# Where the seven-product quads stand in the down projection: the first after eight weight tiles, then one every four

## The chip, the cores and the metric

The kernel runs on one core of a Trainium2 chip. A core has a matrix engine (TensorE, here PE, with PEld for its weight loads), a vector engine (DVE), a scalar engine (ACT), GpSimd (POOL) and a queue that mostly starts transfers (SP). PE multiplies 128x128 weight blocks with up to 512 columns and adds into PSUM banks. The engines run side by side and wait for one another through semaphores. The metric is the device time of one execution in microseconds (us); the kernel before has a median of 2102.93 us over 3 runs (2102.6 to 2103.97).

## The reference

One transformer-like block on 256 tokens of width 2048, in float32: a feed-forward part, a mixer, and a second feed-forward part, each with a root-mean-square norm ahead and behind and a residual. Only the feed-forward parts matter here:

```python
D_FF = int(math.ceil(8 * D_MODEL / 3 / 256)) * 256        # 5632

def _swiglu(x, w_gate, w_up, w_down):
    return (jax.nn.silu(x @ w_gate) * (x @ w_up)) @ w_down

f = _swiglu(_rmsnorm(h, ln_ffn1_pre[l]), ffn1_gate[l], ffn1_up[l], ffn1_down[l])
h = h + MACARON_WEIGHT * _rmsnorm(f, ln_ffn1_post[l])
```

The down product takes the hidden values (256 x 5632) times `w_down` (5632 x 2048). The mixer (projections, a recurrent branch, a pooling branch) stands between the two feed-forward parts and is not touched.

## The kernel before, in words

**Precision.** Each float32 operand is split into a high part (a cast to the fast format fp32r) and a low part (the remainder). A product is three matmuls: high by high (line 158), low weights by high (159), high weights by low (160). So every weight tile passes through three engines before PE: a DMA from SP's queue brings it, ACT casts it (tile `wH`, line 134), DVE subtracts the cast from it (tile `wL`, line 135). The raw tiles `w32` have 4 buffers, `wH` and `wL` 5 each (lines 35 and 36): a new DMA waits until the low part of the tile four places before is done, a new cast until PE has finished the tile five places before.

**The feed-forward part.** `ffn` goes through 11 blocks of 512 hidden columns: gate, then up, then the product of the two. `shuffle_split` brings each block into the layout that the down product needs, with 16 small copies on ACT (line 493), a cast to the high part (496) and a subtraction on DVE (497). Then `post` calls `seven` twice, for output columns 0 to 1023 and 1024 to 2047.

**`seven`** forms two 512-column halves, `f` and `l`, for two halves of the tokens. The inner dimension has 44 rows of 128. The last 32 go the plain way, two at a time: `pair` loads one tile (two rows by 512 columns) and does four products of three matmuls, 12 matmuls in all. This text counts such tiles from 0; there are 16 for `f` and 16 for `l`. The first 12 rows go by a Strassen-like scheme, two at a time, in six quads: `quad` does seven products (21 matmuls) in place of eight, into banks named `ms` or `mm`. Each quad takes

- four DMAs of 256 KB into two `w32` buffers (line 279),
- three DVE operations that form differences of the weights, `t13` (283) and `t24` (285, 286),
- four splits, each a cast on ACT (293) and a subtraction on DVE (294): the direct weights, half a tile more, `t13` and `t24`,
- sums of the input, which `sums` makes for two quads at a time: DVE 218 to 228, a cast on ACT (230), DVE 231. In the first call of `seven` they are made for quads 1 and 2 at its start, and for the next ones when the first and third quad are issued. The second call uses them again.

**The order.** In the loops of `seven` a quad is issued behind the tiles whose numbers stand in `QUADS` (line 48): the first list for the `f` loop, the second for the `l` loop, `False` for the first call and `True` for the second. Behind the last quad `merge` combines the seven banks. DMAs stand in SP's queue in the order in which they are issued; on PE, ACT and DVE a scheduler orders the instructions when the program is built, and the splits and weight differences have a high priority (lines 133, 282, 292), the sums and `shuffle_split` none.

Of the kernel before, what the change touches and what calls it, by code (L numbers as in the profile page):

```python
# [44 lines left out]
WARM = 12  # L45
TB = 4
NQ = 6
QUADS = {False: ((4, 9, 14), (2, 5, 8)), True: ((2, 5, 8, 11, 14), (1,))}

ROWS = [("ln_mix_pre", 16), ("ln_ffn2_pre", 16), ("mu", 26), ("w0", 8), ("a0", 8),  # L50
        ("k_k", 8), ("k_a", 8)]
# [3 lines left out]
class Block:  # L55
# [179 lines left out]
    def seven(s, w, cf, cl, at, KT, T, sm, ev_first, ev_last, trail):  # L235
# [29 lines left out]
        def pair(k, c0, b):  # L265
            keep(s.load_w(w, k, 2, c0, 512))
            for i in range(2):
                for h in range(2):
                    mul(f"{b}{h}", rows(k + i, h), ws[k + i])
# [43 lines left out]
        for i, k in enumerate(range(K0, KT, 2)):  # L313
            pair(k, cf, "f")
            if i in QUADS[trail][0]:
                quad(next(q))
# [16 lines left out]
        for i, k in enumerate(tiles):  # L333
            pair(k, cl, "l")
            if i in QUADS[trail][1]:
                quad(next(q))
# [1017 lines left out]
```

## Time and profile before

| | |
|---|---|
| median of 3 runs | 2102.93 us |
| profiled execution, its own time | 2103.1 us |
| its span, first to last instruction | 2101.4 us |
| PE, PEld, DVE, ACT busy | 99%, 83%, 66%, 55% |
| mean granted TensorE clock | 0.994 |
| DMA | 406.99 MB, mean 194 GB/s |
| 24 quads: line 283 on DVE, first and last start | 508.4 us, 2044.7 us |

A row of the profile names the line of the program, the engine, the operation, the output and the inputs without their buffer numbers, and the shape. In a timeline the first column is the start, the second the duration, and a bracket at the end gives the idle time of that engine just before, with what ended it. Matmuls are pipelined: one of 128x512 has a duration of 0.39 us while the next starts after some 0.23. The granted clock is 1.00 at full rate.

### The profile page before, as it was taken

Reading aid. Unit: us, or ns where it says so; the run is one execution under the profiler, and the core shown is the slowest. Engines: PE = TensorE matmul, PEld = TensorE weight load, DVE = VectorE, ACT = ScalarE, POOL = GpSimd, SP = SyncE. Lnnn points to the kernel's source line nnn. Section 1 sums busy time; section 2 is a strip of 40 time slices with the busy share of each in tenths; the row PEclk is TensorE's granted clock in tenths of the full one; section 3 lists DMA queues with packets and bytes.
Section 4 is the critical chain, followed back from the end, with each engine's and each line's share of the span. In section 5 each row is a group of like instructions: output and inputs, shape, how many; then the busy total and the mean of one; then the engine's idle time right before and its main releaser. Section 6 shows DMA issues by size and latency. Waiting matters only on the chain.

```text
span 2101.4 us, 29096 instructions
## 1 busy us (share of the span) xinstructions
PE 2077.6 (99%) x11017; PEld 1748.1 (83%) x11017; DVE 1389.0 (66%) x1776; ACT 1157.0 (55%) x1658; POOL 76.0 (4%) x161
## 2 busy tenths in 40 slices
PE   9999999999999999999999999999999999989998
PEld 7888888887888899999888788888888888878886
DVE  6555555556787765799688666575655555567776
ACT  7565555655555565474466444466555565555543
POOL 0000000000000010000110110010000000000000
PEclk9999999999999999999999999999999999999999
DMA  7656666564667666556456565565665656645674
GB/s 260 194 179 208 194 194 196 178 204 153 207 196 253 222 188 189 177 165 194 133 159 189 160 249 188 194 220 181 197 203 191 192 179 208 195 152 199 205 243 160
DMA packets 224885, 406.99 MB, mean 194 GB/s; under 512 B 13919, under 2 KB 49897, under 8 KB 224745
## 3 DMA queue, kind: packets, MB, share of 16 engines
q1 hardware_dynamic: 218569, 384.69, 57.3%
q0 software_dynamic: 5888, 19.93, 2.6%
q8 instruction: 86, 1.41, 0.3%
q10 hardware_dynamic: 288, 0.52, 0.1%
q14 instruction: 54, 0.44, 0.1%
HBM read 396.69 MB, written 8.39 MB: 193 GB/s over the span
## 4 chain that ended last, share of the span: by engine, by line
PE 95%; DVE 2%; issue 1%; ACT 1%; POOL 0%; DMA 0%; POOLq 0%; DVEq 0%; SPq 0%; ACTq 0%
PE mm L158 26%; PE mm L160 26%; PE mm L159 26%; PE mc L438 10%; PE ms L159 1%; PE ms L160 1%; PE ms L158 1%; ACT x L493 1%; PE tr L466 1%; PE pA L1075 0%; ACT wH L293 0%; PE pSa L1183 0%; DVE sx L218 0%; PE pU L1171 0%; DMA w<-in_ffn_gate_dram 0%
## 5 line engine op out<-in xcount | busy, mean ns | idle before, releaser
L135 DVE TENSOR_TENSOR wL<-w,wH 128x1024 fp32r<-128x1024 f32 (+2 forms) x677 | 811.0, 1209 | 546.2 <-ACT wH L134 542.9
L134 ACT CAST wH<-w 128x1024 fp32r<-128x1024 f32 (+2 forms) x677 | 698.7, 1044 | 634.2 <-PE mm L160 491.9
L160 PE MATMUL mm<-wH,xL 128*128 128x512 f32 x2316 | 902.2, 390 | 0.7 <-DVE xL L474 0.7
L159 PE MATMUL mm<-wL,xH 128*128 128x512 f32 x2316 | 902.0, 389 | 0.0
L158 PE MATMUL mm<-wH,xH 128*128 128x512 f32 x2316 | 897.9, 392 | 0.0
L160 PEld LDWEIGHTS mm<-wH,xL 128*128 128x128 f32 x2316 | 435.1, 188 | 92.4 <-DVE xL L474 1.5
L158 PEld LDWEIGHTS mm<-wH,xH 128*128 128x128 f32 x2316 | 435.7, 188 | 90.3 <-ACT xH L472 0.2
L159 PEld LDWEIGHTS mm<-wL,xH 128*128 128x128 f32 x2316 | 435.4, 188 | 89.5 <-DVE wL L135 0.2
L438 PE MATMUL mc<-xH,wH 128*128 128x256 f32 x560 | 159.5, 285 | 0.0
L438 PE MATMUL mc<-xL,wH 128*128 128x256 f32 x560 | 158.4, 283 | 0.0
L438 PE MATMUL mc<-xH,wL 128*128 128x256 f32 x560 | 158.3, 283 | 0.0
L493 ACT COPY x<-T 32x256 f32<-32x256 f32 x352 | 141.9, 403 | 3.9
L438 PEld LDWEIGHTS mc<-xH,wH 128*128 128x128 f32 x560 | 106.0, 189 | 1.1
L438 PEld LDWEIGHTS mc<-xH,wL 128*128 128x128 f32 x560 | 106.0, 189 | 0.2
L438 PEld LDWEIGHTS mc<-xL,wH 128*128 128x128 f32 x560 | 106.0, 189 | 0.1
L293 ACT CAST wH<-t 128x1024 fp32r<-128x1024 f32 x48 | 50.5, 1051 | 63.0 <-DVE t L286 31.0
L293 ACT CAST wH<-w 128x1024 fp32r<-128x1024 f32 (+1 forms) x48 | 40.2, 838 | 63.7 <-DMA w<-in_ffn_down_dram 45.6
L294 DVE TENSOR_TENSOR wL<-t,wH 128x1024 fp32r<-128x1024 f32 x48 | 58.6, 1222 | 21.3 <-ACT wH L293 21.1
L294 DVE TENSOR_TENSOR wL<-w,wH 128x1024 fp32r<-128x1024 f32 (+1 forms) x48 | 44.7, 953 | 13.6 <-ACT wH L293 13.6
L283 DVE TENSOR_TENSOR t<-w,w 128x1024 f32<-128x1024 f32 x24 | 29.4, 1225 | 27.7 <-DMA w<-in_ffn_down_dram 26.6
L547 POOL DMA_DIRECT2D gb<-in_ln_ffn_post_dram x4 | 2.4, 592 | 1228.2 <-DVE wL L294 1228.2
L512 ACT ACTIVATE sg<-mm,rs 128x512 f32<-128x512 f32 x44 | 29.9, 689 | 22.5 <-PE mm L160 22.4
(284 smaller groups left out, 1510.4 us busy)
## 6 DMA issues: line engine op xcount, KB each, us to landing
w<-in_ffn_up_dram SPq DMA_DIRECT2D x176, 512.0 KB
w<-in_ffn_gate_dram SPq DMA_DIRECT2D x174, 512.0 KB
w<-in_ffn_down_dram SPq DMA_DIRECT2D x128, 512.0 KB
w<-in_w_in_dram SPq DMA_DIRECT2D x128, 512.0 KB
w<-in_ffn_down_dram SPq DMA_DIRECT2D x96, 256.0 KB
w<-in_w_out_dram SPq DMA_DIRECT2D x32, 512.0 KB
w<-in_w_proj_b_dram SPq DMA_DIRECT2D x16, 512.0 KB
w<-in_w_proj_a_dram SPq DMA_DIRECT2D x16, 512.0 KB
```

The costliest lines, as they stand in the source:

```text
L134: s.nc.scalar.copy(vH, v)
L135: s.nc.vector.tensor_tensor(out=vL, in0=v, in1=vH.bitcast(F32), op=ALU.subtract)
L158: nc.tensor.matmul(ps, aH, bH, start=start, stop=False)
L159: nc.tensor.matmul(ps, aH, bL, start=False, stop=False)
L160: nc.tensor.matmul(ps, aL, bH, start=False, stop=stop)
L283: V.tensor_tensor(out=t13, in0=va, in1=vb[:, :1].to_broadcast([P, 2, 512]), op=ALU.subtract)
L293: nc.scalar.copy(H, v)
L294: V.tensor_tensor(out=L, in0=v, in1=H.bitcast(F32), op=ALU.subtract)
L438: s.nc.tensor.matmul(o, lh, rh, start=one and n == 0, stop=k == KT - 1 and n == 2, skip_group_check=True)
L466: nc.tensor.transpose(ps[:, i], src[:, i * P:(i + 1) * P], s.ident)
L493: nc.scalar.copy(dst[q * 32:q * 32 + 32, :, :, i], src[i * 32:i * 32 + 32, :, :, q])
L512: nc.scalar.activation(out=sg, in_=ps, func=AF.Sigmoid, scale=rs[h])
```

## The change

One line. In the first call of `seven` the first quad stands behind tile 7 instead of tile 4, so eight tiles stand ahead of it and not five, and the next two follow after four tiles each instead of five. In the `l` loop the three quads stand behind tiles 3, 6 and 9 instead of 2, 5 and 8. Counted over both loops, the gaps ahead of the six quads were 5, 5, 5, 4, 3 and 3 tiles, with seven tiles behind the last; they become 8, 4, 4, 4, 3 and 3, with six behind it. The second call is as it was. Both feed-forward parts use the same table.

```diff
-QUADS = {False: ((4, 9, 14), (2, 5, 8)), True: ((2, 5, 8, 11, 14), (1,))}
+QUADS = {False: ((7, 11, 15), (3, 6, 9)), True: ((2, 5, 8, 11, 14), (1,))}
```

The loops that read it are in `seven`:

```python
for i, k in enumerate(range(K0, KT, 2)):
    pair(k, cf, "f")
    if i in QUADS[trail][0]:
        quad(next(q))
...
for i, k in enumerate(tiles):
    pair(k, cl, "l")
    if i in QUADS[trail][1]:
        quad(next(q))
        if left["p1"] == 0:
            merge()
```

## The prediction

> **What bounds the kernel now.** I read the page first, then the waits of PE, then PE's own timeline at the place that the waits name.
>
> ```profile
> span 2101.4 us, 29096 instructions
> PE 2077.6 (99%) x11017; PEld 1748.1 (83%) x11017; DVE 1389.0 (66%) x1776; ACT 1157.0 (55%) x1658; POOL 76.0 (4%) x161
> ```
> ```profile
> PE ms L158 <- ACT wH L293: 5.7, 4, 1.8
> PE mm L158 <- ACT sH L230: 4.2, 2, 2.1
> ```
>
> PE is the bound. It waits for almost nothing, and its largest waits are of two kinds, L293 (cast of a quad's weights) and L230 (cast of a sum's operand), with counts of 4 and 2. The program has 24 quads, so these can belong to two of them only. The timeline of PE shows which: the first quad of FFN1's down product, and that of FFN2.
>
> ```profile
> 503.63 0.39 PE L158 MATMUL ms<-wH,xH 128*128 128x512 f32 x1
> ...
> 504.77 0.39 PE L160 MATMUL mm<-wH,xL 128*128 128x512 f32 x1
> 507.25 0.55 PE L158 MATMUL mm<-wH,sH 128*128 128x512 f32 x1 [2.09 <-ACT sH L230]
> ...
> 510.78 1.22 PE L158 MATMUL ms<-wH,sH 128*128 128x512 f32 x2 [1.47 <-ACT wH L293]
> 513.24 0.79 PE L158 MATMUL ms<-wH,sH 128*128 128x512 f32 x1 [1.24 <-ACT wH L293]
> ...
> 518.20 0.39 PE L159 MATMUL mm<-wL,xH 128*128 128x512 f32 x1
> ```
> ```profile
> 1865.35 0.39 PE L160 MATMUL mm<-wH,xL 128*128 128x512 f32 x1
> ...
> 1879.86 0.40 PE L159 MATMUL mm<-wL,xH 128*128 128x512 f32 x1
> ```
> Busy time by windows (columns: length, then PE, PEld, DVE, ACT, POOL, granted clock, DMA share, GB/s); a count includes a matmul that runs into the window.
> ```profile
> 490.02:503.62 13.60, 13.60 (x61) 11.26 (x60) 6.84 (x9) 10.04 (x20) 0.00 (x0) 1.00 0.27 78
> 505.20:518.00 12.80, 7.75 (x17) 4.83 (x18) 11.62 (x17) 7.05 (x8) 0.00 (x0) 0.60 0.30 84
> 1865.80:1879.60 13.80, 8.23 (x19) 5.52 (x20) 12.62 (x18) 8.07 (x8) 0.00 (x0) 0.63 0.30 106
> ```
>
> Undisturbed, 60 matmuls start in 13.60 us: 0.2267 us each. From 504.77 to 518.20 there are 13.43 us for 18 steps, which need 4.08: 9.35 us lost. In FFN2, 14.51 us for 20 steps (4.53): 9.98 lost. Together 19.3 us, some of it idle, some at a granted clock of 0.5:
>
> ```profile
> 504.15:507.56 3.41, 1.32 (x6) 0.80 (x5) 2.23 (x6) 1.04 (x1) 0.00 (x0) 1.00 0.00 0
> ...
> 514.39:517.80 3.41, 3.41 (x10) 2.63 (x9) 3.41 (x5) 2.68 (x3) 0.00 (x0) 0.50 0.41 133
> 517.80:521.21 3.41, 3.41 (x17) 2.81 (x16) 3.41 (x4) 2.10 (x2) 0.00 (x0) 1.00 0.89 304
> ```
> ```profile
> 1862.66:1866.07 3.41, 3.07 (x14) 2.22 (x12) 3.29 (x5) 0.05 (x1) 0.00 (x0) 1.00 0.00 0
> 1866.07:1869.48 3.41, 1.13 (x3) 0.48 (x3) 2.26 (x4) 1.04 (x1) 0.00 (x0) 1.00 0.00 0
> ```
>
> The rate changes at steps of 3.41 us: after a stretch with 2.09 or 2.28 us idle it is halved, after one with 0.34 idle not, and it comes back after a full one.
>
> Why the quad is late, on ACT and DVE:
>
> ```profile
> 492.95 1.05 ACT L293 CAST wH<-w 128x1024 fp32r<-128x1024 f32 x1 [1.66 <-PE mm L160]
> 493.91 6.63 ACT L493 COPY x<-T 32x256 f32<-32x256 f32 x16
> 500.56 0.62 ACT L293 CAST wH<-w 128x512 fp32r<-128x512 f32 x1
> ...
> 506.15 1.04 ACT L230 CAST sH<-sf 128x1024 fp32r<-128x1024 f32 x1 [4.02 <-DVE sf L228]
> 509.68 1.05 ACT L293 CAST wH<-t 128x1024 fp32r<-128x1024 f32 x1 [2.48 <-DVE t L283]
> 512.14 1.04 ACT L293 CAST wH<-t 128x1024 fp32r<-128x1024 f32 x1 [1.42 <-DVE t L286]
> ```
> ```profile
> 494.04 1.22 DVE L294 TENSOR_TENSOR wL<-w,wH 128x1024 fp32r<-128x1024 f32 x1 [0.55 <-ACT wH L293]
> ...
> 503.31 1.22 DVE L218 TENSOR_TENSOR sx<-xH,xL 128x1024 f32<-128x1024 f32 x1
> 504.56 0.43 DVE L223 SCALAR_TENSOR_TENSOR sf<-sx 128x256 f32<-128x256 f32 x1
> ...
> 507.23 1.22 DVE L231 TENSOR_TENSOR sL<-sf,sH 128x1024 fp32r<-128x1024 f32 x1 [1.11 <-ACT sH L230]
> 508.37 1.22 DVE L283 TENSOR_TENSOR t<-w,w 128x1024 f32<-128x1024 f32 x1
> 509.62 0.69 DVE L285 TENSOR_TENSOR t<-w,t 128x512 f32<-128x512 f32 x1
> ...
> 511.37 0.69 DVE L286 TENSOR_TENSOR t<-w,t 128x512 f32<-128x512 f32 x1
> ...
> 513.78 1.22 DVE L294 TENSOR_TENSOR wL<-t,wH 128x1024 fp32r<-128x1024 f32 x1
> ...
> 515.25 2.36 DVE L135 TENSOR_TENSOR wL<-w,wH 128x1024 fp32r<-128x1024 f32 x2
> ```
>
> Sixteen copies of the last hidden block hold ACT until 500.56; the sums of the first input block and the differences of the weights follow in one row on DVE and end at 512, 8 us after the quad was due.
>
> **The change, part by part.** No instruction is added or removed; the order moves. Three more tiles (12 matmuls, 2.72 us each) stand ahead of the first quad: it is due at 503.63 + 8.16 = 511.79. In the order of the built program ACT now casts tiles 6 and 7 behind the copies, then the hidden block, then the quad's direct weights; DVE has the low parts of tiles 6 and 7, L497, L218, two L294 (one of half size), and then the same chain. Steps by the rows: one cast after another 0.96 (492.95 to 493.91), cast to its low part 1.09, a full DVE operation 1.14 (507.23 to 508.37), a half one 0.61 (0.69 less the same overlap of 0.08).
>
> - ACT: 500.56 and 501.52 tiles 6, 7; 502.48 hidden block; 503.44 and 504.40 the quad's direct weights, 7 us before they are due.
> - DVE: 501.65, 502.79 low parts; 503.93 L497; 505.07 L218 (before 503.31, so only 1.76 later); 506.21, 507.35 the two L294; 507.96 L223.
> - L223 to the cast of the sums 1.59, to L231 1.08: 510.63, ahead of need. The waits for L230 and L231 go.
> - L283 1.14 later, 511.77; its cast 1.31 later, 513.08; PE may use it 1.10 later (509.68 to 510.78): 514.18. PE has done nine matmuls by 511.79 + 2.04 = 513.83. Wait: 0.35.
> - L285 1.25 after L283, L286 1.75 after that: 514.77. Its cast 0.77 later, PE 1.10 later (512.14 to 513.24): 516.64, where PE would come at 514.64. Wait: 2.00. This is what is late next; a wait for L293 stays.
> - The low part of these weights begins 2.41 after L286, that of tile 8 1.47 after that, and is there 1.22 later: 519.87; PE wants it twelve matmuls after 516.64, at 519.36. Wait: about 0.54.
>
> So 2.89 us per FFN stay where 9.35 and 9.98 were, before the clock. The stall of 2.00 leaves PE idle for about 1.84 (a matmul still runs 0.39). That lies between 0.34 (kept) and 2.09 (halved), much nearer the second, but the boundary of the 3.41 us steps may cut it in two. A halved step does 10 matmuls in place of 17 by the rows above: 7 x 0.2267 = 1.6 us, of which 0.54 replaces the last wait: 1.05 net. Bounds per FFN: 0 (no step halved) and 1.05 + 1.6 (two steps). I take one net price for the two FFNs together.
>
> In the Trainium skill, "TensorE: Matmul & The Clock Gate", Part 1 on the clock gate, the half rate comes after at least one idle window of about 3.4 us. By that rule nothing is halved here, and the sum is 1.05 less; but by that rule the 2.09 us above would not have halved it either, and they did.
>
> **SP's queue, POOL and the later quads.** The quad's four DMAs go behind those of tiles 5 to 7, when the low parts of tiles 4 and 5 free their buffers, at 495.3 the latest (494.04 + 1.22); they have 8 us until the cast at 503.44 and cost nothing; without that cover, the queue's wait would be PE's. Tiles 8 and 9 are fetched at 503 and 504. For the second quad, now four tiles behind the first and not five, the rows of the same quad before are:
>
> ```profile
> 517.63 2.27 SPq L279 DMA_DIRECT2D w<-in_ffn_down_dram  x4
> ```
> ```profile
> 524.12 1.23 DVE L283 TENSOR_TENSOR t<-w,w 128x1024 f32<-128x1024 f32 x1 [1.65 <-DMA w<-in_ffn_down_dram]
> ```
>
> The last of its DMAs was issued at 519.5 and L283 began 4.6 later. After: tile 9's low part ends at 521.0, the last issue is at 521.4, L283 at 526.0; two full and two half operations and one more full one (4.64) to L286, 0.77 and 1.10 to PE: 532.5. PE comes there at 511.79 + 4.76 + 2.89 + 10.88 + 2.49 = 532.8. Slack 0.3 us: hidden, barely; with a late DMA up to some 2 us show. What speaks for cost nothing: the fourth to sixth quads before stand four and three tiles apart, and the counts of waits above leave none for them. The merge (six tiles follow it, not seven: 16.3 us for nine operations of at most 1.22) and POOL's loads, whose order is the same, I take as hidden too.
>
> **Sum.** 19.33 - 2 x 2.89 - 1.05 = 12.5 us gained. The profiled execution takes 2103.1 (span 2101.4 and 1.7 around it): 2090.6. The median shown is 0.17 less: 2090.4.
>
> **Rivals.**
> - No halved step in either FFN: 1.05 better, 2089.4. For it: 1.84 idle is under 2.09 and can be cut by a boundary. Against: it is near 2.09. The page named above would give this.
> - Both FFNs are halved, for one or two steps: 2091.5 to 2094.7. For it: if 1 us of idle is enough, nearly every position of the boundary halves it.
> - The second quad is late: DMAs that land 2 us later take the slack and 1.7 of PE's time, and perhaps a halved step, in each FFN: 5 us, 2095.7. For it the slack of 0.3; against it the rows of the three-tile spacing.
> - The chain moves with the quad, because the scheduler puts the sums as late as before relative to the quad: 2102.9. The built order speaks against it: L218 moves by 1.76 us, the quad by 8.16.
> - Slower: the second and third quads, four tiles apart, both wait for weights, since each takes two of the four buffers and the next fetch cannot begin. It decides from 6.3 us per FFN on (12.5 / 2), that is L283 some 6.5 us later than I have it; there it is 2102.9, and with three halved steps as before, some 3 us net in each FFN, 2109. Against: the longest wait needs a DMA that lands in over twice the 4.6 us seen.
>
> **Numbers.** Forecast 0.36; no halving 0.20; both halved 0.25; second quad late 0.12; moves along 0.03; slower 0.04. 0.2% of the time, 4.2 us, is about what a measurement can tell from no change. Faster 0.93, same 0.03, slower 0.04. Low end: both FFNs with the 2.00 wait alone, 15.3 gained, 2087.6, rounded down for a chain a little quicker than replayed to 2087.2. High end: both halved for two steps with 0.4 us of the second quad, 2095.0; what lies above is most of the last three cases.
>
> **What would show it.** After: PE's waits for L230 and L231 gone at both quads, one wait of about 1.8 us for L293 at each, near 514.6 in FFN1; the quad's first product at 511.8; a granted clock of 0.5 for at most one or two steps of 3.41 us behind it; no wait of PE in the second to sixth quads. Wrong it would be if DVE starts L283 of the first quad much off 511.8, or if PE waits for L293 or L294 near 532.

## The result, and the profile after

The changed kernel takes 2090.43 us in the median (2089.97 to 2091.84), the kernel before, run beside it, 2102.89 us. The ratio is 0.9941, with a 95% interval of 0.9924 to 0.9958. A second set of executions, against 2102.48 us before, gives 2090.69 us and a ratio of 0.9942 (0.9928 to 0.9956). The profiled execution took 2090.64 us, 12.46 less than the one before.

The waits of PE at the quads of the changed kernel (us in total, times, longest):

```profile
PE ms L158 <- ACT wH L293: 3.8, 4, 1.7
...
PE mm L159 <- DVE wL L135: 0.5, 2, 0.2
```

The waits for L230 and L231, the operands made from the sums, are gone. What is left is L293, the cast of the quad's weights. PE's timeline at the first quad of FFN1 and of FFN2:

```profile
512.55 0.39 PE L158 MATMUL ms<-wH,xH 128*128 128x512 f32 x1
...
514.37 0.39 PE L160 MATMUL mm<-wH,sL 128*128 128x512 f32 x1
514.91 0.73 PE L158 MATMUL ms<-wH,sH 128*128 128x512 f32 x2 [0.16 <-ACT wH L293]
517.39 0.50 PE L158 MATMUL ms<-wH,sH 128*128 128x512 f32 x1 [1.74 <-ACT wH L293]
...
520.65 0.50 PE L159 MATMUL mm<-wL,xH 128*128 128x512 f32 x1 [0.25 <-DVE wL L135]
520.98 0.39 PE L160 MATMUL mm<-wH,xL 128*128 128x512 f32 x1
...
1868.66 0.39 PE L160 MATMUL mm<-wH,sL 128*128 128x512 f32 x1
...
1875.28 0.40 PE L160 MATMUL mm<-wH,xL 128*128 128x512 f32 x1
```

From 514.37 to 520.98 there are 6.61 us for 16 matmuls, which need 3.63 at 0.2267: 2.98 lost, and in FFN2 (1868.66 to 1875.28) 2.99. Before it was 9.35 and 9.98, so the two quads give back 13.36 us. The chain on ACT, and that on DVE:

```profile
494.67 6.63 ACT L493 COPY x<-T 32x256 f32<-32x256 f32 x16
...
513.81 1.06 ACT L293 CAST wH<-t 128x1024 fp32r<-128x1024 f32 x1 [2.48 <-DVE t L283]
516.29 1.04 ACT L293 CAST wH<-t 128x1024 fp32r<-128x1024 f32 x1 [1.43 <-DVE t L286]
```
```profile
505.81 1.22 DVE L218 TENSOR_TENSOR sx<-xH,xL 128x1024 f32<-128x1024 f32 x1
...
511.36 1.23 DVE L231 TENSOR_TENSOR sL<-sf,sH 128x1024 fp32r<-128x1024 f32 x1 [1.12 <-ACT sH L230]
512.50 1.22 DVE L283 TENSOR_TENSOR t<-w,w 128x1024 f32<-128x1024 f32 x1
513.75 0.69 DVE L285 TENSOR_TENSOR t<-w,t 128x512 f32<-128x512 f32 x1
514.36 1.22 DVE L218 TENSOR_TENSOR sx<-xH,xL 128x1024 f32<-128x1024 f32 x1
515.50 0.68 DVE L286 TENSOR_TENSOR t<-w,t 128x512 f32<-128x512 f32 x1
...
517.23 0.42 DVE L223 SCALAR_TENSOR_TENSOR sf<-sx 128x256 f32<-128x256 f32 x1
517.57 0.41 DVE L227 TENSOR_TENSOR sf<-sx 128x256 f32<-128x256 f32 x1
...
525.39 1.23 DVE L283 TENSOR_TENSOR t<-w,w 128x1024 f32<-128x1024 f32 x1
```

The chain still starts with the sixteen copies and still runs through the sums into the differences of the weights. The quad's first product starts 8.92 us later (503.63 before, 512.55 now), and the chain's last cast begins 4.15 us later (512.14 before, 516.29 now); 0.75 us of both come from the start of the execution, as shown below, so that the quad moved by some 8.16 and the chain by 3.4. The 3.4 us are the length of three full operations on DVE (at 1.14 from one to the next, 3.42): the three tiles that now stand ahead of the quad need their low parts made there.

Between L285 and L286, the two halves of t24, stands L218 of the next sums. It does nothing for this quad, and L286 waits for it. L223 and L227 are of the same sums. The description of the kernel before has these sums made when the first quad is issued; by the condition in `quad`, `len(sm) < min(q + 2, n)`, they are issued with the second and the fourth quad, and the scheduler put them this far ahead. The last row is the second quad: DVE comes to it with no wait for a DMA.

The 13.36 us at the quads are 0.90 more than the whole execution gained. The down product of FFN1, which in the profile before begins with the matmul at 490.04, begins here at 490.79:

```profile
490.04 0.39 PE L158 MATMUL mm<-wH,xH 128*128 128x512 f32 x1
```
```profile
490.79 0.39 PE L158 MATMUL mm<-wH,xH 128*128 128x512 f32 x1
```

So 0.75 us were lost ahead of everything that the change moves, and the trace shows where. Two matmuls at the start of the changed kernel's execution:

```profile
8.73 0.63 PE L159 MATMUL mm<-wL,xH 128*128 128x512 f32 x1
...
10.93 0.39 PE L159 MATMUL mm<-wL,xH 128*128 128x512 f32 x1
```

The first takes 0.63 us, as matmuls do in the halved steps; in the profile before, the same matmul starts at 8.28 and takes 0.40. The second starts at 10.20 there, 0.73 sooner, and from there on the distance hardly changes. It differs between executions of one kernel: the 61st matmul starts at 16.02 in the profile before, at 16.79 here and at 17.15 in the second profile of the changed kernel. The other 0.15 are spread over the rest.

### The profile page after: what moved, and what is told of

It reads as the page before. It is cut to its first block, busy times and chain, and to the rows that moved or that the text cites. A ratio compares the mean times of both kernels' runs of the same rounds, so it can differ in the third digit from the quotient of the medians.

```text
span 2088.9 us, 29095 instructions
## 1 busy us (share of the span) xinstructions
PE 2072.3 (99%) x11017; PEld 1745.5 (84%) x11017; DVE 1387.7 (66%) x1776; ACT 1156.1 (55%) x1658; POOL 76.0 (4%) x161
## 4 chain that ended last, share of the span: by engine, by line
PE 95%; DVE 2%; issue 2%; ACT 1%; POOL 0%; DMA 0%; POOLq 0%; DVEq 0%; ACTq 0%
PE mm L158 26%; PE mm L159 26%; PE mm L160 26%; PE mc L438 10%; PE ms L159 1%; PE ms L160 1%; PE ms L158 1%; PE tr L466 1%; ACT x L493 1%; PE pA L1075 0%; DVE wL L135 0%; DVE wL L294 0%; PE pSa L1183 0%; DMA x<-in_x_dram 0%; DVE sx L218 0%
## 5 line engine op out<-in xcount | busy, mean ns | idle before, releaser
L293 ACT CAST wH<-t 128x1024 fp32r<-128x1024 f32 x48 | 50.5, 1053 | 64.2 <-DVE t L286 47.9
L293 ACT CAST wH<-w 128x1024 fp32r<-128x1024 f32 (+1 forms) x48 | 40.0, 838 | 58.8 <-DMA w<-in_ffn_down_dram 48.3
L283 DVE TENSOR_TENSOR t<-w,w 128x1024 f32<-128x1024 f32 x24 | 29.4, 1224 | 23.7 <-DMA w<-in_ffn_down_dram 22.1
```

Of the source, the lines that this page charges most:

```text
L283: V.tensor_tensor(out=t13, in0=va, in1=vb[:, :1].to_broadcast([P, 2, 512]), op=ALU.subtract)
L293: nc.scalar.copy(H, v)
```

## The experiments

The theory under test: the first quad waits because the copies of the last hidden block, the sums and the quad's own differences stand in one chain on ACT and DVE, and the later place gives that chain time. The main rivals: the new distances between the later quads bring the gain; the copies alone, or the sums alone, are what is late; transfers are late; and, for what remains, what the clock does with a gap of 2 us. Each kernel was compared with the kernel before on the same chip.

**Only the places of the later quads.**

```diff
-QUADS = {False: ((4, 9, 14), (2, 5, 8)), ...
+QUADS = {False: ((4, 11, 15), (3, 6, 9)), ...
```

> Only the second half of the change: the first quad stays behind the fifth weight tile, and the five later quads stand where the change puts them. Theory (the gain is the first quad's own wait: its operands, the sums of the last hidden block, come late): nothing is gained, the first quad of each FFN loses the 9.35 and 9.98 us of before again, 2102.9 us (2101.5 to 2104.5). Rival (the spacing of the later quads brings the gain): about 2090.4 us, and the loss at the first quad is unchanged while some wait of the later quads is gone.

Measured: 2103.69 us against 2103.09, ratio 1.0001 (0.9992 to 1.001). The waits of before are all there:

```profile
PE ms L158 <- ACT wH L293: 6.0, 5, 1.8
PE mm L158 <- ACT sH L230: 4.2, 2, 2.1
```

The first quads lose 9.4 and 10.0 us. The later places alone give nothing; this rival falls.

**Only the first quad's place.**

```diff
-QUADS = {False: ((4, 9, 14), (2, 5, 8)), ...
+QUADS = {False: ((7, 9, 14), (2, 5, 8)), ...
```

> Only the first half of the change: the first quad behind the eighth tile, the second still behind the tenth, so that two tiles and not four stand between them. Theory: the losses at the first quad are those of the changed kernel (3.0 us per FFN in its profile); the second quad, two tiles closer, waits up to 0.6 us for its cast of t24, 2090.4 + 2 x 0.3 to 0.6 = 2091.0 to 2091.7 us (2089.8 to 2093). Rival (the later spacing is needed, since the second quad collides with the first one's splits): 2.6 us or more is lost at each second quad, 2095.7 us or above. Rival (the spacing alone gives the gain): 2102.9 us.

Measured: 2091.89 us, ratio 0.9947 (0.9935 to 0.996). PE's timeline at the second quad:

```profile
526.96 0.61 PE L158 MATMUL ms<-wH,sH 128*128 128x512 f32 x2
528.09 0.50 PE L158 MATMUL ms<-wH,sH 128*128 128x512 f32 x1 [0.52 <-ACT wH L293]
```

The first quad's place carries nearly the whole gain, 11.2 us. With only two tiles between the first quads the second one loses 1.13 - 2 x 0.2267 = 0.68 us per FFN, 1.4 for both; by 1.2 to 1.5 us this kernel is behind the changed one. The rival by which a close second quad costs 2.6 us or more falls: even at half the changed kernel's distance it is 0.68.

**The first sums made early, the quads in their old places.** All that the first sums need is done long before the last hidden block. `sm` is handed from `ffn` to `post`:

```diff
+EARLY = 8
...
+        sm = []
...
             while s.after:
                 s.after.pop(0)()
+            if b == EARLY:
+                s.sums(hT, sm)
-        s.post(wd, s.T_at(hT), NKF, gpost, 0.5, resid, emit, reload, hT)
+        s.post(wd, s.T_at(hT), NKF, gpost, 0.5, resid, emit, reload, hT, sm)
...
-            sm = []
```

> The quads stand as in the kernel before; the first sums of each FFN (sf, sH, sL of hidden blocks that are long done) are made after the ninth hidden block instead of after the last one. Theory (the first quad waits for the casts and differences of the sums queued behind the last block's 16 copies, and for its weights' splits queued behind these sums on ScalarE and VectorE): with the sums out of that queue the waits at the first quad shrink to 0.5 to 1.5 us per FFN, the clock there stays whole, 2102.9 - 2 x (9.67 - 1.0) = 2085.6 us (2084.5 to 2088). Rival (the last block's 16 copies on ScalarE are what is late, the sums ride along): the splits still wait for ScalarE, 4 to 5 us per FFN remain, 2093 us or above. Rival (the four DMAs of the quad's weights are late): no change, 2102.9 us.

Measured: 2091.32 us (2089.07 to 2091.97), ratio 0.9941 (0.9929 to 0.9954). That is 5.7 us above what the theory expected and below the rivals. The waits shrink, but not to 0.5 to 1.5 us per FFN. ACT, DVE and PE at the first quad of FFN1, and PE in FFN2 (lines here are one or more higher than in the kernel before):

```profile
494.90 6.62 ACT L494 COPY x<-T 32x256 f32<-32x256 f32 x16
...
508.06 1.04 ACT L294 CAST wH<-t 128x1024 fp32r<-128x1024 f32 x1 [1.40 <-DVE t L287]
```
```profile
503.14 1.23 DVE L498 TENSOR_TENSOR xL<-x,xH 128x1024 fp32r<-128x1024 f32 x1 [0.26 <-ACT xH L497]
504.29 1.22 DVE L284 TENSOR_TENSOR t<-w,w 128x1024 f32<-128x1024 f32 x1
...
506.15 1.22 DVE L219 TENSOR_TENSOR sx<-xH,xL 128x1024 f32<-128x1024 f32 x1
507.29 0.68 DVE L287 TENSOR_TENSOR t<-w,t 128x512 f32<-128x512 f32 x1
```
```profile
506.70 0.73 PE L159 MATMUL ms<-wH,sH 128*128 128x512 f32 x2
509.15 0.53 PE L159 MATMUL ms<-wH,sH 128*128 128x512 f32 x1 [1.72 <-ACT wH L294]
...
513.14 0.39 PE L160 MATMUL mm<-wL,xH 128*128 128x512 f32 x1
...
1862.11 0.73 PE L159 MATMUL ms<-wH,sH 128*128 128x512 f32 x2
...
1868.18 0.40 PE L161 MATMUL mm<-wH,xL 128*128 128x512 f32 x1
```

From 506.70 to 513.14 twelve matmuls take 6.44 us and need 2.72: 3.7 lost. In FFN2 fifteen matmuls from 1862.11 to 1868.18 take 6.07 and need 3.40: 2.7 lost. The gap is the same; in FFN1 a step of half clock follows, which is shown further below.

What I had overlooked: with the sums gone, the quad's first difference (here L284) stands on DVE right behind the low part of the last hidden block (L498), which waits for that block's cast and so for the sixteen copies. The copies hold the quad's weights back although these need no copy. And the next sums' difference, here L219, stands ahead of L287 as in the changed kernel. The last cast begins at 508.06; before, at 512.14, with the copies 0.99 us earlier. So the sums are worth 4.08 + 0.99 = 5.07 us of the chain; in the kernel before they stand on DVE from L218 at 503.31 to L283 at 508.37, 5.06.

**One copy in place of sixteen for the last hidden block, the quads in their old places.**

```diff
-        for i in range(4):
+        whole = j == NKF // 4 - 1
+        if whole:
+            nc.scalar.copy(x32.rearrange("p k s -> p (k s)"), T1)
+        for i in range(0 if whole else 4):
```

This kernel leaves out the order of the block's pieces, so that only its time can be used.

> The quads stand as in the kernel before; the last hidden block of each FFN is written by one copy of 128x1024 in place of the 16 copies that put its 32-row pieces in their places, so that the block's order is left out (the values are those of the block, in other places). This shortens ScalarE's queue ahead of the sums by 6.63 us less about 0.95 us, and leaves the sums where they are. Theory (copies and sums stand in one chain, and either's 5.7 us cuts what the first quad waits for): 1.3 to 2 us per FFN remain, the clock stays whole, 2102.9 - 2 x 8.1 = 2086.7 us (2085.5 to 2089). Rival (the sums' chain alone sets it): the first quad still loses 5 us or more per FFN, 2094 us or above.

Measured: 2088.61 us, ratio 0.9932 (0.992 to 0.9945), near the upper end of what the theory expected. ACT and PE at the first quad:

```profile
494.44 1.05 ACT L493 COPY x<-T 128x1024 f32<-128x1024 f32 x1
...
507.06 1.04 ACT L293 CAST wH<-t 128x1024 fp32r<-128x1024 f32 x1 [1.41 <-DVE t L286]
```
```profile
508.16 0.50 PE L158 MATMUL ms<-wH,sH 128*128 128x512 f32 x1 [1.35 <-ACT wH L293]
```

The last cast begins 5.08 us earlier than before, and the copies began 0.53 later, so 5.61 us came out of the chain; the copies' own rows say 6.63 - 1.05 = 5.58. Copies and sums stand one behind the other: taking out either shortens the chain by its own length, and neither alone empties it. The rivals that name one of them alone fall.

**The next sums behind the quad's own differences.** The changed kernel, with two lines moved from the start of `quad` to its end:

```diff
-            if len(sm) < min(q + 2, n):
-                s.sums(T, sm)
...
             mul("l1", rows(k + 1, 1), t4)
+            if len(sm) < min(q + 2, n):
+                s.sums(T, sm)
```

> The changed kernel, but the sums for the next quads are issued after a quad's own differences and splits instead of ahead of them. Theory (the 1.7 to 1.9 us that remain before p6 are the cast of t24 standing on VectorE and ScalarE behind the next quads' sums): that wait shrinks to about 0.8 us and the 0.6 us behind it go, 2090.4 - 2 x 1.8 = 2086.8 us; later quads may wait some tenths for sums that come later (up to 1.7 us per FFN more), so 2086 to 2090 us. Rival (the wait before p6 is that of the weights' transfers): no change, 2090.4 us or above.

Measured: 2087.38 us, ratio 0.9926 (0.9913 to 0.9938). On DVE nothing stands any more between the two halves of t24 (here L283 and L284), and PE's wait is a microsecond shorter:

```profile
513.34 0.69 DVE L283 TENSOR_TENSOR t<-w,t 128x512 f32<-128x512 f32 x1
514.07 0.69 DVE L284 TENSOR_TENSOR t<-w,t 128x512 f32<-128x512 f32 x1
```
```profile
515.97 0.50 PE L158 MATMUL ms<-wH,sH 128*128 128x512 f32 x1 [0.74 <-ACT wH L291]
```

So 1.0 (1.74 less 0.74) of the 2.03 us that remain in the changed kernel is the price of one operation of other work, L218, in the middle of the quad's chain. The 0.5 behind it are gone too. For them L218 alone is not enough, since PE itself goes on 1.0 earlier: L223, L227 and L225 of the same sums stood ahead of the low part of the next tile in the changed kernel, at 517.23, 517.57 and 519.04, some 0.34 each, and here they do not. At the first quad the transfers are not what is late.

**The first quad behind the seventh, the ninth and the tenth tile.**

```diff
+QUADS = {False: ((6, 11, 15), (3, 6, 9)), ...
+QUADS = {False: ((8, 12, 15), (3, 6, 9)), ...
+QUADS = {False: ((9, 12, 15), (3, 6, 9)), ...
```

The seventh:

> The changed kernel with its first quad behind the seventh tile instead of the eighth, one tile of 2.72 us earlier but its DMAs, casts and sums issued as much earlier in the program only where the queues let them. Theory (the wait is set by the chain of copies and sums, whose end moves little): the waits grow from 2.7 to about 4.3 us per FFN, 1.76 us before p5 and 1.91 us before p6 with 0.3 us of work between; with no halved clock 2090.4 + 2 x 1.6 = 2093.6 us (2092.5 to 2095). Rival on the clock (some 3.7 us idle out of 4 us halve it for a step or two of 3.41 us, as 4.9 us before did for three): 1.05 to 3.4 us more per FFN, 2095.7 to 2100.4 us, and the granted clock at the first quad reads below 1.

The ninth:

> The changed kernel with its first quad behind the ninth tile and three tiles before the second. Theory: the waits shrink from 2.7 to about 1.2 us per FFN (0.5 us for the cast of t24 and 0.6 us for the split of the next tile), 2090.4 - 2 x 1.6 = 2087.2 us (2086 to 2088.5). Rival (the residual wait for t24 goes along with the quad, since the sums of the next quads are issued with it): 2090.4 us. Rival (the second quad, a tile closer, now waits): above 2088.5 us with waits at the second quad.

The tenth:

> The changed kernel with its first quad behind the tenth tile and three tiles between the quads. Theory: nothing of the first quad's chain is late any more, no wait over 0.3 us at any quad, 2090.4 - 2 x 3.0 = 2084.4 us (2083.5 to 2086). Rival (the last quad, behind the sixteenth tile, or the closer spacing brings new waits): 2087 us or above. Rival (the residual wait moves with the quad): 2090.4 us.

Measured, with the loss at the first quads from PE's timelines as above:

| first quad behind tile | time, us | ratio (95%) | lost in FFN1, FFN2 |
|---|---|---|---|
| 5 (before) | 2103.29 | 1 | 9.35, 9.98 |
| 7 | 2096.19 | 0.9964 (0.995 to 0.9977) | 5.6, 6.8 |
| 8 (changed) | 2090.43 | 0.9941 (0.9924 to 0.9958) | 2.98, 2.99 |
| 9 | 2086.59 | 0.9922 (0.991 to 0.9934) | 1.4, 1.4 |
| 10 | 2084.33 | 0.9912 (0.9899 to 0.9926) | 0, 0 |

From the eighth tile to the ninth the quad is due 2.72 us later, and 1.6 less are lost: the chain moves by the other 1.1, again about one DVE operation for the tile that now stands ahead of it. So a tile is worth some 1.6 us and not 2.72. Behind the tenth nothing is left to gain at the first quads. The theory's times hold at the ninth and the tenth tile, the rivals there fall. At the seventh it is the rival on the clock that holds: by 1.6 per tile 4.6 would be lost, and the halved steps bring the rest. PE's busy time and granted clock by its steps of 3.41 us (columns: length, busy, granted clock, DMA share, GB/s):

```profile
509.76:513.17 3.41, 1.72 (x8) 1.00 0.00 0
513.17:516.58 3.41, 1.66 (x6) 1.00 0.65 159
516.58:519.99 3.41, 3.41 (x10) 0.50 0.50 158
```

One step is halved here, in FFN1, and two are in FFN2. In the profile of the kernel with the tenth tile the first quads lose nothing, but one quad of FFN2's last pass loses 3 us between 2018 and 2024, behind a difference on DVE that had waited 4.03 us for a transfer; the theory had no wait over 0.3 us at any quad. No kernel here moves that quad within its pass. This execution took 2086.77 us; the other three took 2083.93 to 2084.53.

**The changed kernel with the early sums.**

> The changed kernel and, beside it, the first sums made after the ninth hidden block. Theory (what remained of the wait with the early sums alone was the last block's copies and its own difference ahead of the quad's differences, and the two differences of the next sums; the later place of the quad hides these): no wait over 0.3 us at any quad, as with the first quad behind the tenth tile, 2084.3 us (2083.5 to 2086). Rival (with the sums early, the quad's own chain simply moves with its place): 2 us and more per FFN remain, 2088 us or above.

Measured: 2084.0 us, ratio 0.9911 (0.9898 to 0.9925), with no wait of PE at any quad. The two remedies meet at the same floor as the tenth tile. This kernel and that one beat both the kernel before and the changed one.

**The changed kernel once more, for the clock.**

> The changed kernel once more, for the granted clock. Theory (the clock is halved for a 3.41 us step when the idle time within one step before it is 2.0 us or so, and the place of the steps against the program differs from one execution to the next): in this profile the 2.03 us gap before p6 either lies across the bound of two steps, with no halved clock and 3.0 us lost, or within one, with one halved step of 3.41 us behind it and 4.0 to 4.7 us lost; over the executions 2089.7 to 2093.5 us. Rival (a gap of 2.03 us never halves it): 3.0 us at both quads and all executions within 0.5 us of 2090.2 us but for the start.

Measured: 2090.69 us (2089.61 to 2092.23); the losses in its profile are 3.0 and 3.0, with no halved step. Here the gap at the first quad of FFN1 lies within one step, and yet the clock stays whole, while the early-sums kernel above has a halved step in FFN1 and none in FFN2 with the same gap. The changed kernel again, then the early-sums kernel:

```profile
515.91:519.32 3.41, 1.66 (x8) 1.00 0.68 213
519.32:522.73 3.41, 3.19 (x15) 1.00 0.46 130
```
```profile
506.08:509.49 3.41, 1.69 (x7) 1.00 0.57 152
509.49:512.90 3.41, 3.41 (x10) 0.50 0.45 156
...
1861.17:1864.58 3.41, 1.69 (x8) 1.00 0.42 141
1864.58:1867.99 3.41, 3.13 (x13) 1.00 0.54 167
```

So both sides of this experiment are too simple. A gap of this size can halve the clock, against the rival; and lying within one step is not enough, against the theory. The executions lie 2.6 us apart; halved steps and the start would be enough for that, but of the other four there is no trace, and where they lost or won time is not shown.

## Why the prediction was right, step by step

- **The quad is due 8.16 us later, the chain only a little.** Right. All times here are 0.75 us later than predicted because of the later start. Less that, L218 began at 505.06 (predicted 505.07), L231 at 510.61 (510.63), L283 at 511.75 (511.77), and the quad's first product at 511.80 (511.79).
- **What is late next.** Right: the cast of t24. The three losses were predicted as 0.35, 2.00 and 0.54 (for the last, its own steps give 519.87 less 519.36, that is 0.51). They are 0.31 (514.37 to 514.91, less one matmul), 2.03 (514.91 to 517.39, less two), and 0.41 ahead of the 520.65 row; the first matmul behind each longer gap is also about 0.1 late, which the sum had left out. 2.98 and 2.99 in place of 2.89.
- **One halved step, 1.05 net.** This is the term that failed: the profiled execution has none. The price was right, as the early-sums kernel shows: 3.7 lost with a halved step, 2.7 without. Its chance was not. In the changed kernel the bound of two steps, reckoned back from where the clock falls at the end of the program (2082.6), lies at 515.87 and at 1870.96, inside the gap both times, and cuts it into steps that are busy enough:

```profile
512.46:515.87 3.41, 3.03 (x13) 1.00 0.09 5
515.87:519.28 3.41, 1.89 (x8) 1.00 0.66 216
...
1867.55:1870.96 3.41, 2.23 (x9) 1.00 0.22 69
1870.96:1874.37 3.41, 2.69 (x12) 1.00 0.68 238
```

That was named in the prediction as what could undo the step; I gave it too little weight. And a gap need not be cut to be harmless: in the profiles with a gap of this size (the changed kernel twice, the first quad's place alone, the early sums) one of eight gaps was followed by a halved step. "No halving" had a chance of 0.20 in the prediction, which by these few is too low.
- **The second quad, slack of 0.3 us.** Right that it is hidden, but its transfers came sooner than reckoned: L283 began at 525.39, or 524.64 less the start, where I had 526.0. The rival in which its transfers land 2 us later did not come about, and even at half the distance the loss was 0.68 per FFN.
- **The chain moves with the quad; slower.** The rows exclude both. The chain moved by 4.15 - 0.75 = 3.4 us, the quad by 8.16.
- **The sum.** 12.5 predicted, 12.46 measured in the profiled executions, but agreement this close is luck. At the quads the gain was 13.36: 1.05 more for the step that was not halved, 0.19 less for the small terms. The start then took 0.75, ahead of anything that the change moves, and 0.15 went elsewhere; the two errors nearly cancel. The mechanism and the waits that stay were right without luck.
- **Why the quad is late.** The prediction said: the copies, then the sums and differences in one row. The early-sums and one-copy kernels bear this out, 5.07 and 5.61 us. What the prediction had not seen is that the differences of the weights are held behind the copies even without the sums.

## What to carry to other kernels

When PE waits for an operand of a step whose inputs are made just before it, compare two moves in the trace: how far the step's due time moves, and how far the chain behind the operand moves with it in the order of the other engines; only the difference is gained. Here a tile ahead of the quad moved PE by 2.72 us and the chain by 1.1, since the tile needs an operation on the chain's own engine. Then look along that chain for work that belongs to a later step, for it can be moved by itself: here four operations of the next sums in the wrong place cost 1.5 us in each feed-forward part. And ask whether the step's inputs can be made earlier at all, since that reached the same floor without moving PE's work further.

## What the runs showed of the hardware

The granted clock changes at the bounds of steps that run through the whole execution without regard to the program. In the early-sums kernel it falls at 509.49 and, at the end, at 2083.04: 1573.55 us, 461 steps of 3.4133. In the kernel with the seventh tile it falls at 516.58 and at 2090.14: 461 steps again. The place of the grid against the program differs between the executions. The Trainium skill, "TensorE: Matmul & The Clock Gate", Part 1, has such a free-running window of 3413 ns, and the traces agree.

What I had not expected is how fine the edge is. Of the steps at full rate with 1.66 to 1.72 us busy by the traces, about half, two were followed by a halved one (1.66 with the seventh tile and 1.69 with the early sums) and five were not: 1.66 in the changed kernel's second profile, 1.69 with the early sums, 1.72 with the seventh tile, 1.67 with the first quad's place alone, and 1.67 at the end of the one-copy kernel. In the changed kernel's first profile the steps had 1.89 us busy or more, and none was halved. The Trainium skill has in "TensorE: Matmul & The Clock Gate", Part 1, that the half rate comes after at least one idle window. Here that is not needed: a step half busy was enough twice. Ends of matmuls are modelled in these rows, so that a few hundredths in the busy time mean nothing; what decides at the edge stays open.
